# Two decoder layers on one core: linear attention's values and gates become 1024-column units of an ordered instruction list

## The chip, the core and the metric

The kernel runs on one core of one Trainium2 chip. The metric is the time of one execution in microseconds of device time; less is better. Three runs of the kernel before gave 2152.7, 2152.89 and 2154.03 us, median 2152.89.

## What is computed

Two layers over 256 tokens of width 2048, all in float32. One input projection feeds two groups of heads, gated linear attention (chunks of 64 tokens) and stick-breaking attention; their outputs go through one output projection; an MLP with a squared ReLU follows. Cut to what matters here:

```python
def hybrid_layer(x, ...):
    h = rms_norm(x, attn_norm)
    g_q, g_k, g_v, g_gate, g_lr, s_q, s_k, s_v = split(h @ w_in)   # 512 512 1024 1024 16 1024 1024 1024
    log_a = log_sigmoid(g_lr @ w_gate_up + b_gate) / 16
    o_gla = rms_norm(gla_chunked(g_q, g_k, g_v, log_a), gla_out_norm) * silu(g_gate)
    o_sb = rms_norm(stick_breaking_attention(norm(s_q), norm(s_k), s_v), sb_out_norm)
    x = x + concat(o_gla, o_sb) @ w_o
    return x + square(relu(rms_norm(x, mlp_norm) @ w_up)) @ w_down
```

## The kernel before, in words

**Matmuls.** Every float32 operand is split into a high part and a low part of the reduced matmul type: ScalarE copies the high part (`high`, L966 in the list, L570 outside), VectorE subtracts it from the original (`low`, L970 and L571). A product is then three matmuls: high by high, high by low, low by high. Each weight matrix is read once, in blocks of 1 MB.

**Units of the list.** `listed` (L786) handles most of the work as *units* of 1024 output columns and 2048 rows. A unit goes over 8 *pairs*, each of 2 x 128 rows. A plain pair is 2 row blocks x 2 halves of the columns x 2 token halves, so 8 products or 24 matmuls, in two steps of 12. A *quick* pair is multiplied as a 2 x 2 block matrix with 7 products, so 21 matmuls, in four steps; for it VectorE first adds weight blocks (`t13`, `t2`, `t4` in `steps`, L985), the activations need extra sums (`forms`, L429), and after the last quick pair of a unit the partial results are combined (`sums_of`, L1094, and `finals`, L1117). Which pairs are quick stands in `FAST` and `QUICK` (L410, L413), the order of the pairs in `HEADS` and `ORDER`. Step numbers k count through a unit; dictionaries such as `TURNS` say behind which step a piece of other work is put on TensorE.

**The planner.** A list is built as pieces with an engine, a length and dependencies (`Plan`, L40). TensorE's and SP's pieces keep their given order; VectorE's and ScalarE's get due times counted back from TensorE's order and are run in order of due time. The result is written out as a fixed order of instructions on TensorE, VectorE and ScalarE. SP (the DMA queue) and POOL (GpSimd), and the place of a list's instructions among those traced before it, are left to the framework's scheduler.

**One layer in time.** (1) A list for the keys (`sk`) and values (`sv`) of stick-breaking; for layer 0 it is the front list, for layer 1 the tail of layer 0's list. (2) The attention stage, written without a planner: `unit` (L576, 512 columns or less, 96 matmuls for 512) and `unit_t` (L599, transposed output) for the low-rank gate, the queries of stick-breaking, and the linear attention's queries and keys. Each takes 1/8 or 1/4 of its rows and then ticks a counter; `after(n, fn)` hangs a piece of attention work n ticks ahead. `sb_heads(1, ..., (6, 10))` (L1653) is the second half of stick-breaking: scores of its two pairs of heads at ticks 6 and 10, weights 3 ticks later, outputs 1 later, the turned operand 3 later. (3) Still in this manner: the linear attention's values as two units of 512 columns, the turning of the decayed keys (`turn_k`), `gla_pair` (states and scores of a pair of heads, L1693) and `gla_out` (outputs, L1735), and the first half of the gates as a unit of 512 columns. (4) The layer's list: the second half of the gates as kind `"g"` (96 plain matmuls), the gate functions (`gate`, L1256: three logs' steps, a minimum, an exponent, a product for each token half), the output projection as two units `o`, then eight units `up` and `down` of the MLP in turn, then `sk` and `sv` of the next layer.

**Memory.** `acts` is a pool of 19 tiles of 4 KB per partition for activations, the residual `xb` has 4 such tiles of its own (L341) and stays on the chip throughout. Temporary pools of the attention stage and of the lists share one range of addresses; a new tile there waits for the old ones it lies on. The four newest weight blocks have a place (`RAWS`), their split parts five (`RING`).

The lines that set the sets of quick pairs and the stage's values:

```python
413     QUICK = (((5, 6), (5, 6, 7)), ((4, 5, 6), (4, 5, 6)))      # layer 0: sk, sv; layer 1: sk, sv
805     units = [("sk", 0, 0), ("sv", 0, 0)] if front else [("g", 0, 0), ("o", 0, 0), ("o", 0, 1)]
1759    for g in range(2):
            v = values(unit(hT, wl, 0, C_GV + g * 512, 512), tmp("v4", [P, NT, 512], bufs=2))
            for hp in range(2):
                after(1 + 3 * hp, lambda e=2 * g + hp, v=v, c=hp * 2 * P: gla_pair(e, v, c))
        ug = unit(hT, wl, 0, C_GG, 512)
```

Of the kernel before, what the change touches and what calls it, by code (L numbers as in the profile page):

```python
# [10 lines left out]
F32 = mybir.dt.float32  # L11
# [140 lines left out]
def trunk_kernel(  # L152
# [27 lines left out]
    xpool = ctx.enter_context(tc.tile_pool(name="resid", bufs=1, side="right"))  # L180
    apool = ctx.enter_context(tc.tile_pool(name="acts", bufs=19))
# [42 lines left out]
    ATT = ("v4", "tri", "nones", "wg", "reset", "gmask", "mask16", "lr", "lrT", "ha", "hh", "hl", "hA", "on", "dec", "S", "kdz", "row", "bc")  # L224
# [21 lines left out]
    ident16 = cpool.tile([P, P], BF16, name="ident16")  # L246
    kdz = {}
    lc = {}

    def layer_constants():  # L250
        for key in ("tri", "nones"):
            lc[key] = tmp(key, [P, P], F32R, bufs=1)
# [15 lines left out]
        gmask = lc["gmask"] = tmp("gmask", [P, CHUNK], bufs=1)  # L268
        nc.gpsimd.memset(gmask, 1.0)
        for half in range(2):  # L270
# [6 lines left out]
        reset = lc["reset"] = tmp("reset", [P, T], bufs=1)  # L277
        nc.gpsimd.memset(reset, 1.0)
        nc.gpsimd.memset(
            reset.rearrange("p (n c) -> p n c", c=CHUNK)[:, :, 0:1], 0.0  # L280
        )
        kdz["t"] = tmp("kdz", [P, 3, 512], bufs=1)
        nc.gpsimd.memset(kdz["t"], 0.0)

    def build_constants():
        nc.vector.tensor_copy(ident16, ident)

        layer_constants()
# [52 lines left out]
    xb = [xpool.tile([P, NT, 512], F32, name=f"xb{n}") for n in range(4)]  # L341
# [3 lines left out]
    def load_x(n, c=0, w=512):  # L345
        nc.sync.dma_start(xb[n][:, :, c : c + w], xv[:, :, n * 512 + c : n * 512 + c + w])
# [45 lines left out]
    class Operand:  # L392
# [25 lines left out]
    ORDER = {"g": (0, 1, 2, 3), "up": (0, 1, 2, 3, 4, 5, 6, 7), "down": (0, 1, 2, 3, 4, 5, 6, 7)}  # L418

    TURNS = (  # L420
        {1: ((2, 5), (3, 7)), 3: ((1, 1),), 4: ((5, 6), (4, 5)), 7: ((6, 7), (7, 1))},
        {0: ((5, 5),), 1: ((6, 7),), 3: ((4, 1), (7, 6))},
    )
    KEYS = (
        {19: ((0, 0, 5), (0, 1, 7)), 20: ((1, 0, 1),), 21: ((1, 1, 6),)},
        {18: ((0, 0, 5),), 19: ((0, 1, 7),), 20: ((1, 0, 1),), 21: ((1, 1, 6),)},
# [56 lines left out]
    def operand_parts(op, n, h2, key, l, place):  # L483
# [5 lines left out]
        def turn():  # L489
            pt = place()  # L490
            for j in range(2):
                for tt in range(NT):
                    c = (2 * h2 + j) * P
                    nc.tensor.transpose(
                        pt[:, j * T + tt * P : j * T + (tt + 1) * P],
                        xb[n][:, tt, c : c + P], ident,
                    )
# [22 lines left out]
    def norm_squares(n, ssq):  # L520
        for tt in range(NT):
            junk = tmp("t2", [P, 512], bufs=4)
            nc.scalar.activation(
                junk, xb[n][:, tt, :], AF.Square, accum_out=ssq[:, tt, n : n + 1]
# [166 lines left out]
    def sb_scores(qT, kT, h):  # L691
# [11 lines left out]
        for j in range(2):  # L703
            for o in (zA[:, j * T : j * T + P], zB[:, j * P : (j + 1) * P]):
                nc.tensor.matmul(
                    o, ident16, lc["mask16"], start=False, stop=(j == 1), skip_group_check=True
# [79 lines left out]
    def listed(l, front, mixed=None, ons=None, ug=None):  # L786
# [18 lines left out]
        units = [("sk", 0, 0), ("sv", 0, 0)] if front else [("g", 0, 0), ("o", 0, 0), ("o", 0, 1)]  # L805
        fl = l if front else l + 1
        if not front:
            units += [(k, q, n2) for q in range(4) for k in ("up", "down") for n2 in range(2)]
            if fl < DEPTH:
                units += [("sk", 0, 0), ("sv", 0, 0)]  # L810

        def pair_order(u):

            if units[u][0] in HEAD_KINDS:
                i = HEAD_KINDS.index(units[u][0])
                return HEADS[fl][i], set(QUICK[fl][i])
            if units[u][0] != "o":
# [3 lines left out]
            if units[u][2] == 0:  # L821
                return (4, 5, 6, 7, 0, 1, 2, 3), {0, 1}
            return (4, 5, 6, 0, 7, 1, 2, 3), {0, 1}
# [62 lines left out]
        def weights(u, i):  # L886
            kind, q, n2 = units[u]
            if kind in HEAD_KINDS:
                c0 = C_SK if kind == "sk" else C_SV
                src = w_in[fl][2 * i * P : (2 * i + 2) * P, c0 : c0 + 1024]  # L890
            elif kind == "g":
                src = wl[4 * i * P : (4 * i + 4) * P, C_GG + 512 : C_GG + 1024]
# [10 lines left out]
        def load(u, i):  # L903
# [4 lines left out]
            def fn():  # L908
# [4 lines left out]
                dst = box[0]  # L913
                if units[u][0] == "g":
                    dst = dst.rearrange("p k (c n) -> p (k c) n", c=2)
                nc.sync.dma_start(dst, weights(u, i))
# [68 lines left out]
        def steps(u, j, is_fast, r, ld, readers):  # L985
# [3 lines left out]
                "g": hT_now, "o": mixed, "up": hm, "down": up.get(q), "sk": hT, "sv": hT,  # L989
# [5 lines left out]

            if kind == "g":
                for s in range(2):
                    yield parts(
                        lambda s=s: r()[:, s, :].rearrange("p (c n) -> p c n", c=2),
                        readers, ld,  # L1000
                    ), [(m, [(blk(k, tt, 2 * j + s), k) for k in range(2)])
                        for tt, m in enumerate((1, 6))]
                return
# [31 lines left out]
            def fourth():  # L1035
# [16 lines left out]
                (5, [(ext(3) if op is hT or kind == "up" and j == KEPT else blk(0, 1), 0)]), (7, [(ext(2), 1)]),  # L1052
# [31 lines left out]
        def seeds(u):  # L1084

            n2 = units[u][2]
            for m, c, tt in ((2, 0, 0), (4, 0, 1), (3, 1, 0), (8, 1, 1)):
                def seed(m=m, src=xb[2 * n2 + c][:, tt, :]):
                    banks[m] = bank(m)
                    nc.scalar.activation(banks[m], src, AF.Copy)  # L1090
# [40 lines left out]
        def down_tail(u):  # L1131
# [6 lines left out]
            def half(c, p):  # L1138
# [3 lines left out]
                def store(tt):  # L1142
                    if end:
                        nc.sync.dma_start(
                            ov[:, tt, n * 512 : (n + 1) * 512], xb[n][:, tt, :]
# [663 lines left out]
```

## Time and profile before

| | |
|---|---|
| median of 3 runs | 2152.89 us |
| the profiled execution | 2152.91 us |
| its span, first to last instruction | 2151.2 us |
| TensorE, VectorE, ScalarE, GpSimd busy | 100, 88, 65, 2% of the span |
| TensorE's mean granted clock | 0.999 of full speed |
| DMA | 408.98 MB, 55.7% of the 16 engines' time |

The stages lie in the span so: front list 5 to 99 us; layer 0's attention stage to 213, values and first gates to 294, second gates and output projection to 404, MLP to 1082, next keys and values to 1167; layer 1 in the same order, its MLP from 1472 to the end. A row of windows gives, for a stretch, its length and each engine's busy time with the number of instructions, then the granted clock, the share of the DMA engines and GB/s. A row of the chain gives start, length and what the end of the kernel hung on there. A row of lines gives the group and its count, then busy us, mean ns of one, and the idle time ahead of it.

### The profile page before, as it was taken

The numbers are of one execution on the slowest core, as the hardware profiler recorded it, in microseconds if no ns is written. First come the engines' busy times: TensorE is split into PE (matmuls) and PEld (weight loads), VectorE is DVE, ScalarE is ACT, GpSimd is POOL, SyncE is SP. The second block draws the span as 40 slices with busy tenths as digits, with TensorE's granted clock in tenths as the row PEclk, the third lists the DMA queues.
The fourth block names the chain that finished last, engine by engine and source line by source line (L and its number), as shares of the span: only waits on it lengthen the run. The fifth ranks groups of instructions, "written<-read, shape, count | busy, mean of one in ns | idle before, by whom it ended". The sixth has DMA issues, their size and how long they took to land.

```text
span 2151.2 us, 27397 instructions
## 1 busy us (share of the span) xinstructions
PE 2143.1 (100%) x10277; PEld 1787.7 (83%) x10277; DVE 1890.4 (88%) x2355; ACT 1403.8 (65%) x2057; POOL 42.7 (2%) x74
## 2 busy tenths in 40 slices
PE   9999999999999999999999999999999999999999
PEld 7888888888888888888888888888888888888887
DVE  7867569999999899899997775799999999998997
ACT  7676466666576567576666854666665665765674
POOL 0010000000000000000001200000000000000000
PEclk9999999999999999999999999999999999999999
DMA  7554455555556555556655544555555555565564
GB/s 256 159 179 155 157 196 176 193 203 192 199 194 222 188 196 203 208 183 209 208 168 156 181 152 158 192 181 197 212 183 206 205 189 203 191 224 185 196 206 146
DMA packets 136376, 408.98 MB, mean 190 GB/s; under 512 B 6602, under 2 KB 31762, under 8 KB 136244
## 3 DMA queue, kind: packets, MB, share of 16 engines
q1 hardware_dynamic: 136244, 407.24, 55.7%
q8 instruction: 80, 1.31, 0.2%
q14 instruction: 52, 0.43, 0.1%
HBM read 405.12 MB, written 2.10 MB: 189 GB/s over the span
## 4 chain that ended last, share of the span: by engine, by line
PE 94%; ACT 1%; DVE 1%; issue 0%; POOL 0%
PE acc L587 4%; PE acc L593 3%; PE acc L590 3%; PE acc L612 2%; PE acc L616 1%; PE m__623_2954 L1068 1%; PE m__2629_12333 L1068 1%; PE m__2625_12320 L1068 1%; PE m__619_2941 L1068 1%; PE m__2726_12854 L1068 0%; PE m__655_3136 L1068 0%; PE m__2661_12515 L1068 0%; PE m__720_3475 L1068 0%; PE m__2731_12878 L1068 0%; PE m__725_3499 L1068 0%; PE m__2728_12864 L1068 0%
## 5 line engine op out<-in xcount | busy, mean ns | idle before, releaser
L966 ACT ACTIVATE whi<-raw 128x1024 fp32r<-128x1024 f32 (+1 forms) x658 | 684.4, 1056 | 350.9 <-issue 21.1
L970 DVE TENSOR_TENSOR wlo<-raw,whi 128x1024 fp32r<-128x1024 f32 (+1 forms) x658 | 787.6, 1219 | 27.3 <-ACT whi L966 19.0
L571 DVE TENSOR_TENSOR wlo<-raw,whi 128x1024 fp32r<-128x1024 f32 (+2 forms) x128 | 141.7, 1108 | 82.3 <-ACT whi L570 81.1
L966 ACT ACTIVATE whi<-ts 128x1024 fp32r<-128x1024 f32 x129 | 136.6, 1059 | 95.5 <-PE m__1062_5033 L1068 6.5
L970 DVE TENSOR_TENSOR wlo<-ts,whi 128x1024 fp32r<-128x1024 f32 x129 | 158.0, 1225 | 42.5 <-ACT whi L966 42.5
L570 ACT ACTIVATE whi<-raw 128x1024 fp32r<-128x1024 f32 (+2 forms) x128 | 122.0, 954 | 110.7 <-PE acc L593 85.3
L799 DVE TENSOR_TENSOR ts<-raw 128x1024 f32<-128x1024 f32 x129 | 157.6, 1221 | 0.5
L587 PE MATMUL acc<-whi,act 128*128 128x512 f32 (+2 forms) x384 | 140.4, 366 | 0.1
L593 PE MATMUL acc<-whi,act 128*128 128x512 f32 (+2 forms) x384 | 136.5, 356 | 0.0
L590 PE MATMUL acc<-wlo,act 128*128 128x512 f32 (+2 forms) x384 | 136.2, 355 | 0.0
L966 ACT ACTIVATE whi<-t 128x512 fp32r<-128x512 f32 x129 | 80.9, 627 | 49.3 <-DVE t L799 20.2
L970 DVE TENSOR_TENSOR wlo<-t,whi 128x512 fp32r<-128x512 f32 x129 | 88.7, 688 | 9.6 <-ACT whi L966 9.6
L612 PE MATMUL acc<-act,whi 128*128 128x512 f32 x256 | 92.0, 400 | 0.0
L799 DVE TENSOR_TENSOR t<-raw 128x512 f32<-128x512 f32 x129 | 88.9, 689 | 1.1
L799 DVE TENSOR_TENSOR raw<-ts,raw 128x512 f32<-128x512 f32 x129 | 88.6, 687 | 0.3
L587 PEld LDWEIGHTS acc<-whi,act 128*128 128x128 f32 x384 | 72.4, 189 | 13.3 <-issue 2.7
L593 PEld LDWEIGHTS acc<-whi,act 128*128 128x128 f32 x384 | 72.3, 188 | 10.5
L590 PEld LDWEIGHTS acc<-wlo,act 128*128 128x128 f32 x384 | 72.5, 189 | 8.9
L616 PE MATMUL acc<-act,wlo 128*128 128x256 f32 x256 | 71.8, 281 | 0.0
L1199 ACT ACTIVATE act<-act,st 128x512 f32<-128x512 f32 x64 | 44.5, 718 | 32.7 <-DVE act L799 32.7
L612 PEld LDWEIGHTS acc<-act,whi 128*128 128x128 f32 x256 | 48.1, 188 | 10.3
L616 PEld LDWEIGHTS acc<-act,wlo 128*128 128x128 f32 x256 | 48.4, 189 | 0.1
(2583 smaller groups left out, 5480.1 us busy)
## 6 DMA issues: line engine op xcount, KB each, us to landing
raw<-in_w_up_dram SPq DMA_DIRECT2D x128, 1024.0 KB, 5.0
raw<-in_w_down_dram SPq DMA_DIRECT2D x128, 1024.0 KB, 5.3
raw<-in_w_in_dram SPq DMA_DIRECT2D x87, 1024.0 KB, 5.3
raw<-in_w_o_dram SPq DMA_DIRECT2D x32, 1024.0 KB, 5.2
raw<-in_w_in_dram SPq DMA_DIRECT2D x8, 544.0 KB, 3.8
raw<-in_w_in_dram SPq DMA_DIRECT2D x8, 512.0 KB, 3.8
out_dram<-xb SPq DMA_DIRECT2D x8, 256.0 KB, 2.9
xb<-in_x_dram SPq DMA_DIRECT2D x3, 512.0 KB
```

The source lines that it names most:

```text
L570: newest["hi"] = nc.scalar.activation(hi[:, :, :width], r, AF.Copy).ins
L571: newest["lo"] = nc.vector.tensor_tensor(lo[:, :, :width], r, f32(hi[:, :, :width]), ALU.subtract).ins
L587: nc.tensor.matmul(o, xh[:, sl], whi[:, j, :width], start=(k == 0), stop=False)
L590: nc.tensor.matmul(o, xh[:, sl], wlo[:, j, :width], start=False, stop=False)
L593: nc.tensor.matmul(o, xl[:, sl], whi[:, j, :width], start=False, stop=(k == KT - 1))
L612: nc.tensor.matmul(acc[f], whi[:, j, sl], op.both(k), start=(k == 0), stop=False, skip_group_check=True,)
L616: nc.tensor.matmul(acc[f][:, T:], wlo[:, j, sl], xh, start=False, stop=(k == KT - 1), skip_group_check=True,)
L799: nc.vector.tensor_tensor(dst, a, b, op)
L966: nc.scalar.activation(box["h"][:, :n], src(), AF.Copy)
L970: nc.vector.tensor_tensor(box["l"][:, :n], src(), f32(box["h"][:, :n]), ALU.subtract)
L1068: nc.tensor.matmul(o, lhs, rhs, start=start and k == 0, stop=end and i + 1 == len(blocks) and k == 2, skip_group_check=onto,)
L1199: nc.scalar.activation(box[h][:, tt, :], box[h][:, tt, :], AF.Relu, scale=rr[:, tt : tt + 1],)
```

## The change

- The linear attention's values (`gv`) become a third unit of 1024 columns behind `sk` and `sv` in the list ahead of the attention stage, with quick pairs 5, 6, 7 in layer 0 and 5, 6 in layer 1. They stay in two activation tiles until the layer's list.
- Both halves of the gates become one unit `gg` of 1024 columns at the head of the layer's list, with quick pairs 5 and 6.
- The turning of the decayed keys, states, scores, outputs, their norms and the gating become pieces of that list at places that `LINEAR` names.
- The second half of stick-breaking begins at ticks 5 and 8 in place of 6 and 10.
- The residual has no pool of its own; it takes 4 tiles of `acts`, which grows from 19 to 23. It is stored to a buffer in device memory at the end of layer 0, and loaded again ahead of the output projection in both layers (in layer 0 from the input).
- The orders of pairs and turns in the keys', values' and output projection's units are new. The sets of quick pairs there are the same.
- A few constants change pool; `kz`, the cleared tile of turned keys, is filled on POOL at the head of the list.

```diff
-    xpool = ctx.enter_context(tc.tile_pool(name="resid", bufs=1, side="right"))
-    apool = ctx.enter_context(tc.tile_pool(name="acts", bufs=19))
+    apool = ctx.enter_context(tc.tile_pool(name="acts", bufs=23))
...
-    HEAD_KINDS = ("sk", "sv")
-    QUICK = (((5, 6), (5, 6, 7)), ((4, 5, 6), (4, 5, 6)))
+    HEAD_KINDS = ("sk", "sv", "gv")
+    QUICK = (
+        ((5, 6), (5, 6, 7), (5, 6, 7), (5, 6)),
+        ((4, 5, 6), (4, 5, 6), (5, 6), (5, 6)),
+    )
     HEADS = (
-        ((0, 2, 1, 3, 5, 6, 4, 7), (4, 0, 5, 1, 6, 7, 3, 2)),
-        ((0, 2, 5, 3, 6, 4, 1, 7), (6, 0, 7, 5, 4, 1, 2, 3)),
+        ((0, 3, 1, 4, 5, 6, 2, 7), (0, 1, 5, 2, 7, 6, 4, 3), (5, 4, 2, 3, 6, 7, 0, 1), (1, 2, 3, 6, 5, 0, 4, 7)),
+        ((0, 1, 5, 6, 3, 4, 7, 2), (6, 1, 2, 4, 5, 3, 7, 0), (0, 5, 3, 6, 7, 4, 1, 2), (1, 2, 3, 6, 5, 0, 4, 7)),
     )
+    LINEAR = {
+        ('gg', 0, 1): (('k', 0, 6),),
+        ('gg', 0, 2): (('k', 1, 6),),
+        ('gg', 0, 4): (('pair', 3, 1, 6), ('pair', 2, 7, 5)),
+        ('gg', 0, 14): (('out', 2, 1),),
+        ('gg', 0, 15): (('pair', 0, 1, 5),),
+        ('gg', 0, 16): (('out', 3, 7),),
+        ('gg', 0, 17): (('out', 0, 1),),
+        ('o', 0, 0): (('pair', 1, 1, 7),),
+        ('o', 0, 2): (('out', 1, 1),),
+        ('o', 0, 3): (('turn', 0, 7),),
+        ('o', 0, 4): (('turn', 3, 6),),
+        ('o', 0, 6): (('turn', 2, 1), ('turn', 1, 7)),
+    }
+    OUT = ((5, 6, 4, 3, 0, 2, 1, 7), (6, 7, 0, 2, 4, 1, 3, 5))
...
-        units = [("sk", 0, 0), ("sv", 0, 0)] if front else [("g", 0, 0), ("o", 0, 0), ("o", 0, 1)]
+        heads = [(kind, 0, 0) for kind in HEAD_KINDS]
+        units = heads if front else [("gg", 0, 0), ("o", 0, 0), ("o", 0, 1)]
...
+            def half(c, p):
+                for tt, a in enumerate(finals(box, c, p, lambda tt: box[c][:, tt, :])):
+                    def scale(tt=tt):
+                        gates_t[c] = box[c]
+                        nc.scalar.activation(
+                            box[c][:, tt, :], box[c][:, tt, :], AF.Copy,
+                            scale=st["now"][:, tt : tt + 1],
+                        )
+
+                    gate_done[c, tt] = add("ACT", A1, scale, a)
+                gate(c)
...
+            a = add("PE", 6 * 0.112, states, k_done, free[m])
+            b = add("DVE", 0.9, carry, a)
+            free[m] = [b]
+            c = add("PE", 4 * 0.12, scores, free[m2])
+            d = add("DVE", 0.8, masked, c)
+            free[m2] = [d]
...
+            a = add("PE", 1.2, out, b, d, free[m])
+            a = add("ACT", A1 + 2.0, take, a)
+            free[m] = [a]
+            a = add("DVE", 0.2, mean, a)
+            a = add("ACT", 0.4, root, a)
+            a = add("DVE", 0.5, step, a)
+            on_done[e] = add("DVE", V1, lambda: mul_heads(ons[e], ons[e], root_mean, 4), a)
...
+            kd_done = add("DVE", 2.4, None, add("ACT", 1.3, None, add("PE", 0.0, None)))
+            kz = tmp("sx2", [P, 3, 512], bufs=NX["sx", 2])
+            nc.gpsimd.memset(kz, 0.0)
...
+            if kind == "o" and n2 == 0:
+                for n in range(4):
+                    x_done[n] = [add(
+                        "SP", 1.5, lambda n=n: load_x(n, src=xs if l else None), lag=4.6
+                    )]
...
+                if kind == "down" and q == 3 and not end:
+                    held_back.append(lambda: add("SP", 1.5, lambda: store_x(n), x_done[n]))
...
+                if j == order[3]:
+                    while held_back:
+                        held_back.pop(0)()
...
-        sb_heads(1, qT, kTs[1], vs[1], (6, 10))
+        sb_heads(1, qT, kTs[1], vs[1], (5, 8))
```

## Rows read from the trace of the kernel before

**Rows 1.** The page: busy time of the engines, and the chain by engine.
```profile
PE 2143.1 (100%) x10277; PEld 1787.7 (83%) x10277; DVE 1890.4 (88%) x2355; ACT 1403.8 (65%) x2057; POOL 42.7 (2%) x74
...
PE 94%; ACT 1%; DVE 1%; issue 0%; POOL 0%
```
**Rows 2.** Waits of TensorE: who for whom, us in total, times, longest.
```profile
PE m__36_171 L1068 <- ACT whi L966: 1.4, 1, 1.4
...
PE m__36_171 L1068 <- DVE wlo L970: 0.5, 1, 0.5
PE ps L766 <- ACT hA L735: 0.5, 2, 0.2
```
**Rows 3.** Windows by stage of layer 0: PE, PEld, DVE, ACT, POOL, clock, DMA.
```profile
4.92:99.19 94.27, 92.30 (x418) 75.35 (x418) 84.03 (x123) 69.36 (x135) 5.10 (x13) 0.98 0.62 213
99.19:212.65 113.46, 112.94 (x709) 100.04 (x708) 77.96 (x124) 80.25 (x181) 14.46 (x17) 1.00 0.55 172
212.65:294.08 81.43, 81.43 (x463) 66.41 (x461) 43.22 (x71) 37.87 (x76) 1.23 (x4) 1.00 0.47 155
294.08:403.79 109.71, 109.71 (x501) 91.15 (x500) 98.31 (x129) 75.50 (x107) 0.00 (x0) 1.00 0.58 197
403.79:1082.00 678.21, 678.21 (x3073) 563.08 (x3072) 647.07 (x746) 448.66 (x558) 0.00 (x0) 1.00 0.58 199
```
**Rows 4.** Chain in the output projection: first and last of 12 like pieces.
```profile
316.93 1.36 PE m__655_3136 L1068 x6
...
331.89 1.36 PE m__663_3176 L1068 x6
```
**Rows 5.** Chain around a pair of the linear attention in the values' unit.
```profile
267.93 0.81 PE ps L1700 x12
268.74 0.44 PE ps L1717 x8
269.18 0.43 PE acc L587
...
274.86 0.89 PE ps L1742 x8
275.75 1.02 PE ps L1750 x12
```
**Rows 6.** Lines of ScalarE from 212.65 to 340 us, shapes apart.
```profile
L966 ACT ACTIVATE whi<-raw 128x1024 fp32r<-128x1024 f32 x19 | 19.4, 1051 | 7.4 <-PE m__663_3176 L1068 3.1 <-PE m__623_2954 L1068 2.9 <-PE m__658_3152 L1068 1.4
L637 ACT ACTIVATE t<-act 128x128 f32<-128x128 f32 x16 | 4.8, 299 | 0.1
L637 ACT ACTIVATION_READ_ACCUMULATOR t<-act 128x1 f32 x16 | 3.0, 188 | 0.0
...
L1266 ACT ACTIVATE t<-t 128x512 f32<-128x512 f32 x4 | 2.5, 635 | 0.1
...
L756 ACT ACTIVATE act<-ps 128x512 f32<-128x512 f32 x4 | 2.4, 601 | 10.4 <-PE ps L1750 10.4
...
L627 ACT ACTIVATE t<-acc 128x256 f32<-128x256 f32 x2 | 0.8, 380 | 1.5 <-PE acc L616 1.5
```
**Rows 7.** Lines of VectorE from 212.65 to 340 us, shapes apart.
```profile
L970 DVE TENSOR_TENSOR wlo<-raw,whi 128x1024 fp32r<-128x1024 f32 x18 | 21.4, 1221 | 0.6 <-ACT whi L966 0.4
...
L799 DVE TENSOR_TENSOR act<-act,t 128x512 f32<-128x512 f32 x4 | 2.7, 686 | 0.0
...
L629 DVE TENSOR_TENSOR t<-acc,t 128x256 f32<-128x256 f32 x2 | 0.8, 422 | 0.4 <-ACT t L627 0.4
```
**Rows 8.** Timeline of ScalarE ahead of the list (294 us): start, length, idle before.
```profile
288.60 0.60 ACT L756 ACTIVATE act<-ps 128x512 f32<-128x512 f32 x1 [7.78 <-PE ps L1750]
...
291.10 3.90 ACT L966 ACTIVATE whi<-raw 128x1024 fp32r<-128x1024 f32 x4
```
**Rows 9.** Window in the start; columns as in rows 3.
```profile
9.20:12.40 3.20, 3.20 (x9) 2.49 (x8) 1.30 (x2) 2.40 (x7) 0.00 (x0) 0.50 1.03 418
```
**Rows 10.** Waits of SP's queue: its longest in total.
```profile
SPq L916 <- DVE wlo L970: 1413.2, 301, 11.2
```

More of the change, by code (lines that the diff above doesn't have):

```diff
@@ L784, in trunk_kernel, with listed @@
     st = {}
-    def listed(l, front, mixed=None, ons=None, ug=None):
+    def listed(l, front, mixed=None, old=None, linear=None):
         wl = w_in[l]
@@ L1354, in g_tail, with gates_tail, sums @@
-        def g_tail(p):
-            gate_copies(1, lambda tt: banks[(1, 6)[tt]], lambda tt: p[(1, 6)[tt]])
-            for tt, m in enumerate((1, 6)):
-                free[m] = [gate_done[1, tt]]
+        def gates_tail(u):
+            box = {}
+            def sums(p):
+                sums_of(box, p)
+            def half(c, p):
[5 more added lines that the diff above has]
+                            scale=st["now"][:, tt : tt + 1],
+                        )
+                    gate_done[c, tt] = add("ACT", A1, scale, a)
+                gate(c)
+            return sums, half
@@ new lines, in turned_k, with turn, copy @@
+        def turned_k(tt, m):
+            kd = linear[1]
+            def turn():
+                pk = banks[m] = bank(m)
+                for e in range(4):
+                    nc.tensor.transpose(
+                        pk[:, e * P : (e + 1) * P], kd[:, e, tt * P : (tt + 1) * P], ident
+                    )
+            def copy():
+                for half in range(2 - tt):
+                    ps = slice(half * CHUNK, (half + 1) * CHUNK)
+                    nc.vector.tensor_copy(kz[ps, 2 * tt + half, :], banks[m][ps, :])
+            a = add("PE", 4 * TR, turn, kd_done, free[m])
+            k_done.append(add("DVE", 1.2 - 0.6 * tt, copy, a))
+            free[m] = k_done[-1:]
@@ L1470, in listed @@
                         begin = m not in begun
[L1471 to L1474 removed]
+                        end = final if m in (2, 4, 3, 8) else [j] == lasts
                         begun.add(m)
@@ L1549, in trunk_kernel @@
         for c in range(2):
-            vs[c] = values([vs[c]()[:, tt, :] for tt in range(NT)], tmp("v4", [P, NT, 512], bufs=2))
+            vs[c] = values([vs["sv", c]()[:, tt, :] for tt in range(NT)], tmp("v4", [P, NT, 512], bufs=2))
         def sb_heads(g, qT, kT, v, first):
@@ L1759, in trunk_kernel @@
-        for g in range(2):
-            v = values(unit(hT, wl, 0, C_GV + g * 512, 512), tmp("v4", [P, NT, 512], bufs=2))
-            for hp in range(2):
-                after(1 + 3 * hp, lambda e=2 * g + hp, v=v, c=hp * 2 * P: gla_pair(e, v, c))
-        ug = unit(hT, wl, 0, C_GG, 512)
         assert not held
         open_scope("sbuf", mlp=1)
-        kTs, vs = listed(l, False, mixed, ons, ug)
+        kTs, vs = listed(l, False, mixed, vs, (ke, kd, qz))
 _INS = [
```

395 lines of the change are left out of this document (194 added, 201 removed).

## The prediction

> **What bounds the kernel now.** I read the page first. TensorE has instructions in flight for the whole span, and the chain that ended last lies on it for 94% [rows 1]. "Busy" is not enough, since pipelined matmuls cover each other, so I next asked what TensorE waited for: 1.4 and 0.5 us for the first weights, 0.5 us in the two attention stages, and nothing else once the first weights are there [rows 2]. Then the stages [rows 3]: only the front list (94.27 us, TensorE busy 92.30) and the attention stage (113.46 against 112.94) show idle TensorE. In the stretch that the change rewrites (values, gates, output projection) and in the MLP the two figures are equal. VectorE is the next engine: 95% busy in the MLP (647.07 of 678.21 us), yet only 53% in the values stretch (43.22 of 81.43). So the time is the sum of TensorE's work, and an edit is worth what it takes from or adds to that sum, as long as its operands come in time. Last I took the price of that work from the chain of waits: in the list six matmuls of 512 columns advance the end by 1.36 us, in the first piece and in the twelfth alike [rows 4], 0.2267 us each.
>
> The profiled execution took 2152.91 us (span 2151.2, the rest lies around it), the median of three runs is 2152.89; I take the sum from 2152.9.
>
> **Matmuls removed.** Before, values and gates of one layer are four pieces of 512 columns, 96 matmuls each: 384. After, they are two units of 1024 columns with 8 pairs of 24 matmuls, where a quick pair has 7 products of 3, so 21. Layer 0 has three quick pairs in the values and two in the gates (183 + 186 = 369), layer 1 two and two (186 + 186 = 372). The keys' and values' quick sets of stick-breaking stay as large as they were, and so does the output projection's. Gone are 15 + 12 = 27 matmuls, at 0.2267 us **6.1 us**.
>
> The TensorE page of the Trainium skill ("TensorE: Matmul & The Clock Gate", section "Back-to-back issue gap") gives other prices, 216 ns for an isolated gap of 512 columns and about 131 ns sustained; by these the term would be 5.8 or 3.5 us. The trace disagrees with the second: 1.36 us for six, at full clock, is 227 ns, and I stay with it.
>
> **Small matmuls, moved.** States, scores, outputs and transposes of the four head pairs are the same instructions; only their place changes. What a place costs is in the chain [rows 5]: 12 state matmuls 0.81, 8 score matmuls 0.44, then the next big matmul 0.43 instead of 0.23; outputs 0.89 + 1.02, and 0.43 again for the big one behind. Before, eight such entries per layer cost 0.20 us each. After, pairs 3 and 2 stand back to back, so one entry of 0.20 goes; the turning of kd, cut into pieces in the values unit, stands whole in the list. I take the one entry, 0.20 x 2 layers = **0.4 us**; at worst 0, at best twice that.
>
> **VectorE and ScalarE behind it.** Over values, gates and output projection VectorE now does 43.22 + 98.31 = 141.5 us [rows 3]. Out go 32 low-part splits at 1.22 (39.0) [rows 7]. In come, for the gates' unit, 12 splits (14.6), two quick pairs at 3 x 1.22 + 0.69 for their four low parts and 1.22 + 2 x 0.69 for the sums of weights (2 x 6.95 = 13.9), and the unit's combining, 2 x 0.69 + 1.22 + 4 x 0.69 = 5.4: together 33.9. That leaves 136.4 us over a TensorE time of 191.1 - 43.5 (values' 192 matmuls) - 1.4 (the gates' 6) - 0.4 = 145.8 us, 94%. The MLP carries 95% without a wait. ScalarE falls below VectorE: 113.4 - 33.6 (32 splits at 1.05 [rows 6]) - 2.5 (four copies at 0.63) + 20.8 (12 + 6 splits, two of 0.63, one copy) = 98.1 us, 67%. The front list takes the values' unit (about 34 to 39 us of VectorE in 42) with no deadline behind it.
>
> The crowd is local: from the gates' last quick pair to the turn of operand 1 (13 steps, 36 us of matmuls, with pieces and turns 48 us) ScalarE has 13 splits at 1.05, four reads of an output with its squares at 0.60 + 4 x (0.30 + 0.19) = 2.56, and four gate chains of 5 x 0.63 = 3.2, 36.7 us; with roots and operand copies about 41 of 48. The last gate chain after the gates' last matmul is two combines, scale, three logs, minimum, exponent and product, twice for the two token halves, some 10 us; TensorE arrives at the turn that needs it 5 steps and three pieces later, 17.7 us. So it fits, with little to spare. I bound the new waits from below by 0 (the MLP's rows) and from above by one late split (1.05 + 1.22 = 2.3 us) at three places per layer, 13.8 us; nearest is the MLP at 95%, so I take **0.8 us**. Below nothing is excluded, since a wait cannot be negative and the old ones in this stretch were nil.
>
> **Edits at nothing.** Residual in the general pool: 19 tiles + 4 become 23, the same bytes. New transfers: x is read again in both layers and stored once, 2 MB each. They go into SP's queue ahead of the output projection's first weights and, the stores, behind the fourth load of the next keys' unit. At the 418 GB/s of the start [rows 9] that is 5 us of queue per 2 MB. The cover is that the queue waits for buffers, not the other way round: 1413.2 us of SP's waits end with a low-part split [rows 10], and the DMA engines' share in the stretch is 0.58 [rows 3]. If the cover were gone, 5 us per layer. x is needed only at the combining of the output projection's quick pairs, over 40 us later. A load that finds no free tile would hold the weights behind it; by my count of live tiles (11 operand, 4 mixed, 2 + 2 + 2) two are free when the gates begin and every pair used frees more. Masks, kz and per-layer constants on POOL: POOL is 2% busy [rows 1]. The new order of pairs and turns at the start: same loads in the same order; between -1 and +1 us, taken as 0.
>
> **Sum:** 2152.9 - 6.1 - 0.4 + 0.8 = **2147.2 us** (-0.26%). About 0.2%, 4.3 us, is what a measurement of this kernel can tell from no change; faster means below 2148.6, slower above 2157.2.
>
> **Rivals.** *A, slower: the seam behind the key projection.* In the kernel before, ScalarE idled 7.78 us at the end of the gates' first half and then took the last output's read before the list's first split [rows 8]. After, what stands last in front of the list is the joining of the keys, which waits for TensorE's last key matmul. If the list's splits queue behind it, TensorE waits in each layer for two copies (0.38 each [rows 6]), two adds (0.42), two products (0.69) and the low split (1.22) [rows 7]: 4.2 us end to end. Against it: the first split had a reason of its own to be late, its buffers lay over values that the last output still read; now nothing read late lies there. At the start the granted clock stood at 0.50, the 1.2 GHz level, from 9.2 to 12.4 us [rows 9], after TensorE's waits of 1.4 and 0.5 us, which cost half of 3.2 us. The same here makes 5.8 us per layer, 2152.9 - 6.5 + 11.6 = 2158.0. It decides from 5.4 us per layer on. The same page of the Trainium skill (Part 1) says that an idle TensorE falls back to 1.2 GHz; the trace agrees at the start, and shows waits of 0.2 us without it.
> *B: the gates' chain is late.* If the last chain stands behind the first gates' 6.4 us and two reads in ScalarE's queue, turn 3 comes 2 to 4 us late per layer: 2146.4 + 2 x 3 = 2152.4. For it speaks the crowd above, against it the list's order, which is computed by due times.
> *C: stick-breaking's last two pairs*, whose scores start one and two steps earlier, make the second pair's scores and the first pair's weights meet in one step, where they share banks. One late exponent there costs what the two waits of [rows 2] and a read of the bank do, 1 to 2 us per layer: 2149.4.
> That the matmuls don't go is no rival: their number is fixed by the sets of quick pairs.
>
> **How the numbers follow.** Forecast 0.70, A 0.10, B 0.13, C 0.07. Faster: the forecast's 0.70 and a little of C, 0.71. Slower: A and B's far end, 0.11. Same: 0.18. The range reaches from 2144.8 (no new waits, 1 us gained at the start, the small matmuls' best) to 2152.6 (all of C, half of B); outside are A, half of B and a few chances below. The forecast's own range is 2144.8 to 2148.6.
>
> **What would show it.** The list's matmuls still 1.36 us per six; TensorE's waits no longer than now, none behind the key projection; VectorE near 94% from gates to output projection; in the old units' lines 96 matmuls of 512 columns per layer, where 384 stand now. Wrong would be: a clock below 1.00 after 14 us, ScalarE idle before the first gate split, a wait of TensorE for a gated operand, or a front list that grows by more than the 41.5 us of its new unit.

## The result and the profile after

The changed kernel takes 2161.32 us (median of 7 runs, 2158.94 to 2163.17), the kernel before in the same comparison 2153.62 (7 runs, 2152.63 to 2154.12): ratio 1.0035, 95% interval 1.0024 to 1.0047. The forecast was 2147.2, faster, in a range of 2144.8 to 2152.6. The change is slower by 7.7 us, its fastest run lies above the slowest of the kernel before, and the prediction was wrong.

The profiled execution of the changed kernel has a span of 2159.6 us, 8.4 more than before. The page, as in [rows 1]:

```profile
PE 2142.6 (99%) x10250; PEld 1786.5 (83%) x10250; DVE 1943.1 (90%) x2429; ACT 1421.0 (66%) x2079; POOL 41.5 (2%) x71
```

The 27 matmuls are gone (10277 to 10250), VectorE does 53 us more and ScalarE 17. But TensorE is busy for less of a longer span. Its longest waits, where the kernel before has four lines in all (three of them in [rows 2]):

```profile
PE m__38_167 L1079 <- ACT whi L985: 3.3, 2, 1.9
PE m__595_2648 L1079 <- DVE wlo L989: 1.6, 1, 1.6
PE m__2634_12098 L1079 <- DVE wlo L989: 1.6, 1, 1.6
PE ps L562 <- POOL ident masks.py:199: 1.5, 1, 1.5
PE m__595_2648 L1079 <- ACT whi L985: 1.4, 1, 1.4
PE m__2634_12098 L1079 <- ACT whi L985: 1.4, 1, 1.4
PE m__38_167 L1079 <- DVE wlo L989: 0.9, 2, 0.7
PE ps L789 <- ACT hA L758: 0.5, 2, 0.2
PE m__763_3564 L1079 <- ACT m__763_3564 L1101: 0.3, 1, 0.3
```

Two places are new: a second wait in the front list (`m__38`, two times now), and one in each layer (`m__595`, `m__2634`: the first product of the gates' unit, right behind the key projection). The windows by stage of layer 0, columns as in [rows 3]: front list with the values' unit, attention stage, gates and output projection, MLP.

```profile
4.96:147.08 142.12, 137.72 (x601) 112.55 (x601) 120.53 (x159) 92.55 (x160) 1.37 (x3) 0.98 0.61 205
147.08:260.84 113.76, 113.37 (x709) 100.18 (x708) 75.07 (x124) 79.15 (x181) 18.34 (x28) 1.00 0.55 172
260.84:410.60 149.76, 146.46 (x762) 120.38 (x761) 137.14 (x202) 100.39 (x170) 0.00 (x0) 1.00 0.54 184
410.60:1088.80 678.20, 678.20 (x3074) 563.16 (x3073) 647.22 (x746) 449.19 (x558) 0.00 (x0) 1.00 0.58 201
```

The MLP and the attention stage are what they were (678.20 and 113.76 us against 678.21 and 113.46). The front list took 142.12, where 94.27 and the new unit's 41.5 make 135.8: 6.3 too much. Gates and output projection took 149.76, where 145.8 was worked out: 4.0 too much. In layer 1 the same stretch took 151.37, 5.6 too much:

```profile
1329.51:1480.88 151.37, 148.07 (x762) 121.50 (x761) 137.13 (x202) 100.52 (x170) 0.00 (x0) 0.99 0.54 182
```

Inside the list nothing has changed its price. The chain of waits around an output of the linear attention, as in [rows 4] and [rows 5]:

```profile
295.37 1.36 PE m__599_2661 L1079 x6
296.73 0.89 PE m__658_2930 L1471 x8
297.62 1.02 PE m__658_2930 L1479 x12
298.64 1.59 PE m__600_2668 L1079 x6
```

Six matmuls are 1.36 us, the output 0.89 and 1.02, and the entry behind it 0.2.

**The loss at the start.** The timelines of ScalarE and TensorE there (start, length, idle before):

```profile
18.00 0.84 ACT L526 ACTIVATE act<-m__54_231,gcol_a 128x256 fp32r<-128x256 f32 x2 [0.48 <-PE m__54_231 L517]
18.73 1.06 ACT L985 ACTIVATE whi<-raw 128x1024 fp32r<-128x1024 f32 x1
```

```profile
17.36 0.60 PE L517 MATMUL m__54_231<-ident,act 128*128 128x128 f32 x4
19.83 0.53 PE L1079 MATMUL m__38_167<-whi,act 128*128 128x512 f32 x1 [1.88 <-ACT whi L985]
21.09 0.80 PE L1079 MATMUL m__38_167<-wlo,act 128*128 128x512 f32 x1 [0.73 <-DVE wlo L989]
```

The split at 18.73 is the first of the second pair's weights. It stands behind the copy of that pair's own turned operand (`m__54`), and TensorE did that turn at 17.36, directly ahead of the matmuls that need both. So nothing covers a copy, a split and a low split (VectorE's low part of the weights): TensorE starts this pair's matmuls at 19.83 and has the low part at 21.09. In the kernel before the second pair was turned two steps earlier. The time from one matmul's start to the next, above the full-clock step of its shape, summed over the first 50 us (entries of 0.15 us and more), is 11.2 us; before it was 5.0.

Behind this wait the clock falls to half clock (0.50, the 1.2 GHz level), as it did at the start before [rows 9]. It falls again behind layer 1's seam:

```profile
21.69:25.95 4.26, 4.26 (x11) 3.20 (x10) 2.84 (x3) 2.16 (x4) 0.00 (x0) 0.50 0.76 234
1334.28:1337.60 3.32, 3.32 (x9) 2.59 (x8) 3.32 (x4) 0.79 (x2) 0.00 (x0) 0.50 1.00 323
```

**The loss at the seam.** The window behind layer 0's last key matmul, then ScalarE's and VectorE's timelines there:

```profile
260.84:264.35 3.51, 0.77 (x3) 0.19 (x1) 3.02 (x5) 3.51 (x6) 0.00 (x0) 1.00 0.11 19
```

```profile
258.33 0.69 ACT L794 ACTIVATE act<-ps,gcol_b 128x512 fp32r<-128x512 f32 x1 [6.04 <-PE ps L789]
260.81 0.73 ACT L650 ACTIVATE t<-acc 128x256 f32<-128x256 f32 x2 [1.78 <-PE acc L639]
261.43 4.84 ACT L985 ACTIVATE whi<-raw 128x1024 fp32r<-128x1024 f32 x5
```

```profile
261.22 0.77 DVE L652 TENSOR_TENSOR t<-acc,t 128x256 f32<-128x256 f32 x2 [1.41 <-ACT t L650]
262.10 0.69 DVE L1833 TENSOR_TENSOR act<-t,act 128x512 f32<-128x512 f32 x1
262.71 0.68 DVE L1834 TENSOR_TENSOR act<-t,act 128x512 f32<-128x512 f32 x1
263.31 5.76 DVE L989 TENSOR_TENSOR wlo<-raw,whi 128x1024 fp32r<-128x1024 f32 x5
```

ScalarE idles 1.78 us for TensorE's last key matmul, copies, and only then starts the list's splits; VectorE adds and multiplies before the first low split. Between the starts of TensorE's matmuls 1.6 and 1.8 us are lost, 3.4 in each layer. This is rival A, instruction for instruction.

### The profile page after: what moved, and what is told of

The parts are those of the page before. It is cut to its first block, busy times and chain, and to the rows that moved or that the text cites. A ratio compares the mean times of both kernels' runs of the same rounds, so it can differ in the third digit from the quotient of the medians.

```text
span 2159.6 us, 27484 instructions
## 1 busy us (share of the span) xinstructions
PE 2142.6 (99%) x10250; PEld 1786.5 (83%) x10250; DVE 1943.1 (90%) x2429; ACT 1421.0 (66%) x2079; POOL 41.5 (2%) x71
## 4 chain that ended last, share of the span: by engine, by line
PE 97%; DVE 1%; ACT 1%; DMA 0%; issue 0%; SPq 0%; POOL 0%; DVEq 0%; ACTq 0%
PE acc L635 2%; PE acc L610 1%; PE acc L613 1%; PE acc L616 1%; PE acc L639 1%; PE m__2638_12111 L1079 0%; PE m__2639_12118 L1079 0%; PE m__2634_12098 L1079 0%; PE m__600_2668 L1079 0%; PE m__595_2648 L1079 0%; PE m__2728_12607 L1079 0%; PE m__689_3157 L1079 0%; PE m__763_3564 L1079 0%; DMA act<-in_x_dram 0%; PE m__2802_13014 L1079 0%; PE m__599_2661 L1079 0%
## 5 line engine op out<-in xcount | busy, mean ns | idle before, releaser
L985 ACT ACTIVATE whi<-raw 128x1024 fp32r<-128x1024 f32 (+1 forms) x706 | 735.8, 1058 | 391.6 <-issue 28.5
L989 DVE TENSOR_TENSOR wlo<-raw,whi 128x1024 fp32r<-128x1024 f32 (+1 forms) x706 | 843.2, 1215 | 28.9 <-ACT whi L985 20.2
L989 DVE TENSOR_TENSOR wlo<-ts,whi 128x1024 fp32r<-128x1024 f32 x138 | 168.6, 1222 | 41.8 <-ACT whi L985 41.0
L594 DVE TENSOR_TENSOR wlo<-raw,whi 128x1024 fp32r<-128x1024 f32 (+2 forms) x80 | 82.8, 1036 | 40.7 <-ACT whi L593 40.0
L593 ACT ACTIVATE whi<-raw 128x1024 fp32r<-128x1024 f32 (+2 forms) x80 | 71.2, 892 | 47.8 <-PE acc L616 22.9
L610 PE MATMUL acc<-whi,act 128*128 128x272 f32 (+2 forms) x192 | 62.8, 327 | 0.0
L613 PE MATMUL acc<-wlo,act 128*128 128x272 f32 (+2 forms) x192 | 61.5, 320 | 0.0
L616 PE MATMUL acc<-whi,act 128*128 128x272 f32 (+2 forms) x192 | 61.4, 320 | 0.0
L493 DVE TENSOR_TENSOR act<-act,act 128x512 fp32r<-128x512 f32 x64 | 42.4, 684 | 0.0
L489 ACT ACTIVATE act<-act 128x512 fp32r<-128x512 f32 x64 | 39.1, 624 | 0.5
L610 PEld LDWEIGHTS acc<-whi,act 128*128 128x128 f32 x192 | 36.4, 190 | 3.6 <-issue 0.7
```

Of the source, the lines that this page charges most:

```text
L493: nc.vector.tensor_tensor(lo, src, f32(h), ALU.subtract)
L593: newest["hi"] = nc.scalar.activation(hi[:, :, :width], r, AF.Copy).ins
L594: newest["lo"] = nc.vector.tensor_tensor(lo[:, :, :width], r, f32(hi[:, :, :width]), ALU.subtract).ins
L610: nc.tensor.matmul(o, xh[:, sl], whi[:, j, :width], start=(k == 0), stop=False)
L613: nc.tensor.matmul(o, xh[:, sl], wlo[:, j, :width], start=False, stop=False)
L616: nc.tensor.matmul(o, xl[:, sl], whi[:, j, :width], start=False, stop=(k == KT - 1))
```

## The experiments

Times are medians; "stalls" are the sums named above, by the profiled execution. The kernel before had a median from 2152.8 to 2153.0 us in these comparisons.

### e_start: the old order of pairs and turns alone

```diff
-        ((0, 3, 1, 4, 5, 6, 2, 7), ...
+        ((0, 2, 1, 3, 5, 6, 4, 7), ...
-        {1: ((1, 5),), 2: ((2, 7),), 3: ((3, 1),), 4: ((5, 6), (4, 5)), 6: ((6, 7),), 7: ((7, 1),)},
+        {1: ((2, 5), (3, 7)), 3: ((1, 1),), 4: ((5, 6), (4, 5)), 7: ((6, 7), (7, 1))},
```

> The changed kernel with one part undone: in layer 0's keys the pairs and their turns stand again in the order of the kernel before (second pair 2, turned behind step 1), all else as changed; the first two 1 MB weight loads still stand ahead of the second block of x in SP's queue. Theory T (order of turns: the second pair's turn stands right ahead of its matmuls, and the splits of its weights queue on ScalarE behind the copy of that turn): the 2.0 and 1.0 us waits at 17.7 to 21 us and the second half-clock stretch behind them go, the front list ends about 6 us sooner, time about 2155. Theory Q (order of the queue: x's second block comes late because two 1 MB loads went ahead of it): the turn behind step 1 now waits some 3 us for x, the loss moves and does not go, time 2158 to 2161.

Measured: 2163.33 us (2157.89 to 2164.01, 4 runs), no better than the change itself and above what either theory gave; the profiled execution is the fastest of the four, and it has no half clock behind the seams. The waits for weights are gone and one for x has come:

```profile
PE m__46_193 L517 <- DMA act<-in_x_dram: 3.1, 1, 3.1
```

So theory Q's mechanism holds here: the loss moved. The stalls of the first 50 us are 9.1 us. SP's queue in the change and, below it, in the kernel before (start and length of the issue):

```profile
4.18 1.38 SPq L935 DMA_DIRECT2D raw<-in_w_in_dram  x2
5.60 1.08 SPq L345 DMA_DIRECT2D act<-in_x_dram  x2
```

```profile
4.17 0.43 SPq L346 DMA_DIRECT2D xb<-in_x_dram  x1
4.65 0.47 SPq L916 DMA_DIRECT2D raw<-in_w_in_dram  x1
```

Before, x's second block was issued first and the second pair's weights behind it; after, two 1 MB blocks go first. The chain of waits of the changed kernel shows what that costs, from issue to landing:

```profile
5.60 9.83 DMA act<-in_x_dram
```

The Trainium skill ("DMA: Bandwidth & Descriptors", section "Queues, rings and completion order") says that each of the DMA engines takes a ring's descriptors in order; the 9.83 us behind two megabytes agree with that.

### e_spq: the old order of the queue alone

```diff
-        with tc.manual_schedule(engines=MANUAL):
+        with tc.manual_schedule(engines=MANUAL | {mybir.EngineType.SP} if front else MANUAL):
```

> The changed kernel with the other half undone: SP's queue in the front list in the list's own order, so that x's second block stands ahead of the second pair's weights as in the kernel before; pairs and turns as changed. Theory T: the turn of the second pair still stands behind step 3, TensorE still waits about 3 us in front of its matmuls and falls to half clock again, time 2160 to 2161. Theory Q: the loss goes, the front list ends about 6 us sooner, time about 2155.

Measured: 2159.32 us (2156.89 to 2162.39, 9 runs); TensorE waits for no load of x, and its waits for ScalarE's splits are those of the change (`m__38`, 3.3 us in two waits).

Theory T holds here, stalls 9.9 us. Each order by itself is enough to lose most of the time, which is why undoing one shows so little.

### e_startspq: both

It holds both edits above.

> Both of the two edits above in one kernel: pairs and turns of layer 0's keys and SP's queue in the front list as in the kernel before. Both theories: the stalls of the first 50 us are those of the kernel before (about 5.0 us where the changed kernel has 11.2), time about 2155. If the start still lost 3 us or more, neither order would be the cause, and the tiles that x now shares with the operands would be.

Measured: 2157.30 us (2154.41 to 2158.57, 10 runs), 2.3 above the expected 2155; stalls in the first 50 us 4.7, as expected. The start is whole again, and what is left is the seam, with half clock behind it in both layers of this profile: 6.4 us at layer 0's seam and 4.8 at layer 1's.

### e_xown: why the queue changed

```diff
-    apool = ctx.enter_context(tc.tile_pool(name="acts", bufs=23))
+    xpool = ctx.enter_context(tc.tile_pool(name="resid", bufs=1, side="right"))
+    apool = ctx.enter_context(tc.tile_pool(name="acts", bufs=22))
...
-            xt[n] = act_tile(F32, (P, NT, 512))
+            own = n == 1 and src is None and not xt.get(("own", n))
+            xt["own", n] = True
+            xt[n] = xpool.tile([P, NT, 512], F32, name=f"xb{n}") if own else act_tile(F32, (P, NT, 512))
```

> The changed kernel with the keys' pairs and turns of the kernel before (as in the first run), and the second block of x in layer 0 in a tile of its own in place of one of the general pool (22 + 1 tiles); SP's queue left to the framework. With that tile the load of x's second block stands ahead of the second pair's weights again. If the move of the residual into the general pool is what put it behind them, TensorE's wait of 3.3 us for x at 12 us goes and the stalls of the first 50 us are near 5 us: about 4 us less than the run with the turns alone, time 2155 to 2157 (the seams stay as changed). If not, the wait for x stays near 3 us.

Measured: 2157.26 us (2154.59 to 2158.81, 10 runs), 6 less than e_start. In the profiles 3.4 of these are the start (stalls 5.7 us for 9.1); where the others lie was not traced, since e_start's profile is that of its fastest run. SP's queue has x's second block first again:

```profile
4.17 0.44 SPq L348 DMA_DIRECT2D xb<-in_x_dram  x1
4.65 1.52 SPq L938 DMA_DIRECT2D raw<-in_w_in_dram  x2
```

So the move of this block of x into the general pool is what put its load back: from e_start to here nothing but its tile and the pool's size differ. What in the framework's scheduler makes it so was not tried.

### e_seam3: the joining of the keys as a piece of the list

```diff
-            t = join(unit_t(hT, wl, C_GK + b * 256))
+            acc = unit_t(hT, wl, C_GK + b * 256)
+            if b == 1:
+                break
+            t = join(acc)
...
-            kd_done = add("DVE", 2.4, None, add("ACT", 1.3, None, add("PE", 0.0, None)))
+            kd_high = add("ACT", 1.3, join_copies, add("PE", 0.0, None))
+            kd_done = add("DVE", 2.4, join_sums, kd_high)
+            whi[3].append(kd_high)
+            wlo[3].append(kd_done)
...
-        sb_heads(1, qT, kTs[1], vs[1], (5, 8))
+        sb_heads(1, qT, kTs[1], vs[1], (5, 7))
```

> The changed kernel with the joining of the last keys (two copies, two adds, two products) made a piece of the layer's list, placed behind the list's third split, and the second half of stick-breaking one tick earlier in its second pair (5, 7), so that nothing late stands ahead of the splits on ScalarE. The start stays as changed. Theory A (the list's splits queue behind the joining, which waits for TensorE's last key matmul): the two waits of 1.6 and 1.8 us behind the key projection fall to under 0.7 us together in each layer, no half-clock stretch follows in layer 1, time 2161.3 - 2 x 3 - 1.6 = 2153.7, from 2152.5 to 2155. Rival (the first split waits for GpSimd's fills, which end about 259.8 us, or for its weights): the waits stay at 3 us or more, time 2160 to 2162.

Measured: 2154.55 us (2152.61 to 2156.25, 10 runs), 6.8 below the change. TensorE loses 1.2 and 1.4 us at the two seams in place of 3.4, and no half clock follows in the profile, which is of the fastest of these runs. Theory A holds, though the waits do not fall below 0.7. What is left is the first weights themselves:

```profile
257.04 3.91 ACT L985 ACTIVATE whi<-raw 128x1024 fp32r<-128x1024 f32 x4 [3.76 <-DMA raw<-in_w_in_dram]
```

### e_all: the three edits together

It holds the edits of e_start, e_spq and e_seam3.

> The changed kernel with both orders at the start as in the kernel before, and the joining of the last keys as a piece of the list behind its third split (with stick-breaking's second pair one tick earlier). If the two losses add up, start 11.2 to 4.7 us of stalls (-6.5) and the seams 3.4 to 1.3 us per layer with no half-clock stretch (-6.8 measured in the seam's run): 2161.3 - 6.5 - 6.8 = 2148.0, from 2147 to 2149.5, faster than the kernel before. If something else costs time (VectorE's crowd, the transfers of x), it stays above 2150.

Measured: 2149.17 us (2148.50 to 2150.03, 11 runs), ratio to the kernel before 0.9982 (0.9974 to 0.9991). The losses add up, and the change is now faster than the kernel before by 3.8 us. Of the seams 1.0 and 1.4 us are left.

### e_all_r: and the first tiles from the general rings

```diff
-                if x % RAWS < RAWS - 3:
+                if x % RAWS == (0 if front else RAWS - 1):
...
-                if i % RING < RING - 4:
-                    return tmp(f"{tag}{4 + i % RING}", [P, 2, 512], F32R, bufs=1)
-                return part_tile(tag, i % RING - (RING - 4) + part_base, [P, 2, 512])
+                if i % RING == (0 if front else RING - 1):
+                    return tmp(f"{tag}4", [P, 2, 512], F32R, bufs=1)
+                return part_tile(tag, i % RING - (1 if front else 0) + part_base, [P, 2, 512])
```

> As the kernel with all three edits, and in a layer's list the first weight block and the first split parts take tiles of the general rings, the ones that lie over the attention stage's tiles come fourth and fifth. Theory: what is left at the seam (0.2 to 0.4 and 1.0 us) comes from the first weight block, which landed only at 257.0 us, 0.8 us before TensorE was free, since its tile waited for the stage ahead; then the first splits are done before TensorE ends the keys and the rest of the wait goes, 2148 - 2 x 1.2 = 2145.6. Rival: ScalarE and VectorE themselves are late (the join and the stick-breaking operand ahead of the splits), the wait moves to a later split and the time stays at 2148.

Measured: **2145.84 us** (2145.65 to 2147.00, 5 runs), ratio 0.9967 (0.9955 to 0.9980): the fastest of all, faster than both kernels. Three splits of the list now end before TensorE's last key matmul; the timeline of ScalarE has the last two of them, and the joining behind them:

```profile
251.35 2.01 ACT L985 ACTIVATE whi<-raw 128x1024 fp32r<-128x1024 f32 x2 [1.58 <-PE acc L635]
253.90 0.73 ACT L1598 ACTIVATE t<-acc 128x256 f32<-128x256 f32 x2 [0.53 <-PE acc L639]
```

TensorE's waits are those of [rows 2] again, with the seeding of the second output unit added (ScalarE copies x into the banks to which that unit's products are then added):

```profile
PE m__38_167 L1079 <- ACT whi L985: 1.4, 1, 1.4
PE ps L789 <- ACT hA L758: 0.5, 2, 0.2
PE m__763_3564 L1079 <- ACT m__763_3564 L1101: 0.3, 1, 0.3
PE m__2802_13014 L1079 <- ACT m__2802_13014 L1101: 0.3, 1, 0.3
PE m__38_167 L1079 <- DVE wlo L989: 0.2, 1, 0.2
```

The window of its gates and output projection: 146.40 us (145.8 worked out), VectorE 133.38, 91%.

```profile
253.80:400.20 146.40, 146.05 (x763) 120.54 (x762) 133.38 (x199) 96.71 (x166) 0.00 (x0) 1.00 0.55 189
```

### e_r58: without the earlier tick

It is e_all_r with `(5, 8)` again.

> The kernel with four edits, with stick-breaking's second pair at the changed kernel's tick 8 again, so that of the seam's edits only the joining as a piece of the list and the first tiles from the rings are left. Theory: the splits stood behind the joining alone, the tick is not needed, no wait over 0.3 us behind the key projection, 2145.8 within 0.6. Rival: the copy of the last stick-breaking operand, one tick before the end, holds ScalarE as well; then waits of about 1 us per layer come back, 2147.5 to 2148.5.

Measured: 2147.08 us (2146.66 to 2147.82, 7 runs), between the two expected times. The profile has no wait at layer 0's seam, 0.6 us for one low split in layer 1, and 1.0 us more of half clock at the start than e_all_r's. The tick is worth little; the joining and the tiles are the cure. The tiles without the joining were not tried.

### e_all_sp_r: the transfers of x

It is e_all_r with SP's queue in the list's order in every list.

> As the kernel with four edits, with SP's queue in the list's own order in every list, so that the four loads of x (2 MB) come behind the gates' eighth weight block, not among the fifth to eighth. If the transfers of x cost time where they stand (queue and bandwidth ahead of the gates' weights), this is 1 to 2 us faster per layer; if they are covered, as the prediction had it, within 0.7 us of the kernel with four edits.

Measured: 2145.91 us (2145.72 to 2146.29, 5 runs), the same as e_all_r. Where the loads of x stand among the gates' weights costs nothing, as predicted; moving them away altogether was not tried.

### e_onequick and e_gv1: the price of the matmuls

One quick pair in place of two or three, in values and gates on e_all (e_onequick), then in the values alone on e_all_r (e_gv1). The edit of e_gv1; in e_onequick the fourth place, the gates', is `(5,)` in both layers too:

```diff
-        ((5, 6), (5, 6, 7), (5, 6, 7), (5, 6)),
-        ((4, 5, 6), (4, 5, 6), (5, 6), (5, 6)),
+        ((5, 6), (5, 6, 7), (5,), (5, 6)),
+        ((4, 5, 6), (4, 5, 6), (5,), (5, 6)),
```

> As the kernel with all three edits, but with one quick pair in place of two or three in the linear attention's values and in the gates: 6 + 3 matmuls more in layer 0 and 3 + 3 in layer 1, 15 in all, and less work for VectorE. By the price of 0.2267 us, 3.4 us slower than the kernel with all three edits (2151.4 if that is 2148.0). If VectorE's crowd behind the quick pairs cost TensorE time, less than 3.4 us, by 1 us or more.

Measured: 2163.75 us (2161.97 to 2165.91, 4 runs), 14.6 above e_all: not a test of the price. With one quick pair the gates' unit has fewer steps, the pieces of `LINEAR` are keyed by step numbers and land elsewhere, and TensorE waits at new places in both layers' lists, for 1.2 us at the longest. It has e_gv1's wait at L610 (below) as well, and half clock at three places.

> The kernel with four edits, with one quick pair in place of three (layer 0) and two (layer 1) in the linear attention's values: 6 + 3 = 9 matmuls more, at places that nothing else is keyed to. By the price of 0.2267 us per matmul 2.0 us slower, 2145.8 + 2.0 = 2147.9, from 2147.3 to 2148.5. If the quick pairs gave less than their price, because VectorE's added work costs TensorE waits, under 1.2 us.

Measured: 2151.36 us (2151.15 to 2152.54, 11 runs), 5.5 above e_all_r and outside the expected range. Nine matmuls more; the starts of all 512-column matmuls add up to 2.25 us more, near the 2.04 of the price. The other 3.4 us lie in one place that no one planned: with another end of the front list the framework put small work of the attention stage (a row and the gains turned, L570 and L306) ahead of its first unit on TensorE,

```profile
PE acc L610 <- ACT whi L593: 1.2, 1, 1.2
...
PE ps L570 <- POOL bc L569: 0.4, 1, 0.4
```

and half clock followed:

```profile
144.39:147.80 3.41, 3.26 (x15) 2.95 (x15) 0.70 (x3) 0.25 (x1) 0.00 (x0) 0.50 0.51 141
```

### e_out: a quick pair earlier

```diff
-    OUT = ((5, 6, 4, 3, 0, 2, 1, 7), (6, 7, 0, 2, 4, 1, 3, 5))
+    OUT = ((5, 6, 4, 3, 0, 1, 2, 7), (6, 7, 0, 2, 4, 1, 3, 5))
```

> The kernel with four edits, with the last quick pair of the first output projection unit one place earlier (pairs 2 and 1 change places). TensorE's wait of 0.5 us per layer for the seeding of the second unit's bank comes from the first unit's combining, which ends late with only one plain pair behind the last quick one. With two plain pairs behind it the wait goes: 1.0 us faster, about 2144.8. Rival: the seeding waits for x or for ScalarE's own queue, and the wait of 0.5 stays, 2145.8.

Measured: 2149.11 us (2148.61 to 2150.25, 11 runs), 3.3 slower than e_all_r, neither of the expected times. The wait for the seeding is gone, so its cause was right. But the quick pair now meets VectorE earlier, and a low split is late in each layer:

```profile
PE m__2721_12563 L1079 <- DVE wlo L989: 1.2, 1, 1.2
PE m__682_3113 L1079 <- DVE wlo L989: 1.2, 1, 1.2
```

This low split runs at 341 us, some 9 us behind the turn of operand 1 with which the prediction's crowd ended. So VectorE can be late in this stretch, but not at the place that the prediction named.

## Why the prediction was wrong

**The work was sized rightly.** e_all_r does the work of the change without its two accidents, and with the first tiles in another place. Its span is 2143.9 us, 7.26 below the kernel before (2151.2): 6.44 in the starts of 512-column matmuls and 0.82 in the rest. The forecast had 6.1 and 0.4 less, 0.8 more. Its median of 2145.84 lies in the forecast's own range of 2144.8 to 2148.6; e_all, which still has part of the seams' waits, lies 0.6 above that range. The 0.8 us for new waits was worked out from no row, only chosen between bounds; that e_all_r has 1.0 us of them is luck, since they stand at a place that no step named (below). VectorE has 137.1 us from the gates to the output projection in the change, 136.4 were worked out.

**The first step that failed** is "the new order of pairs and turns at the start: same loads in the same order; between -1 and +1 us, taken as 0". The loads were not in the same order, and the turns not early enough: 11.2 - 4.7 = 6.5 us of the profile. The first half could be read in the diff: the second pair's operand is turned behind step 3, right ahead of step 4 that needs it, where it had been behind step 1. The second could only be suspected: x's tiles change pool, and SP's order is left to the framework. The prediction looked at the move of x for its bytes and its cover alone. The two faults also hide each other: undoing one gives 9.1 or 9.9 us of stalls against 11.2.

**The second** is the dismissal of rival A. Its mechanism came, in the place named. The argument against it, that nothing read late lies under the first split's buffers, answers another question: the order of ScalarE's and VectorE's instructions in a list is fixed, the joining stood ahead of it, and in the timeline the first split starts at 261.43, when the copies end. Whether a tile is free does not matter to a split that stands behind the joining. [rows 8] had shown the old ending, in which a copy of an output stood in front of the splits with 7.78 us of idle time ahead of it. The price of A was near: 3.4 us for 4.2, and a half clock that adds from nothing to 3.0 us. e_startspq is rival A alone, 2157.3 us where it was given 2158.0. With the start mended it still makes the change slower than the kernel before, ratio 1.0018 (1.0009 to 1.0027); the chance of 0.10 was too small.

**The sum.** From e_all_r to the changed kernel the span grows by 15.7 us: 6.5 at the start, 3.4 at each seam, 1.6 of half clock behind layer 1's, and the remaining 0.8 in small entries. Against the 7.3 gained, that is the 8.4 lost.

**The rest.** Rival B did not come: no wait of TensorE for a gated operand. Nor C: the waits of stick-breaking are 0.5 us as before [rows 2]. The transfers of x are covered (e_all_sp_r). A wait that no step had is the seeding of the second output unit, 0.5 us per layer in starts of matmuls: the combining of the first unit ends late with one plain pair behind its last quick one. Of the list of what would show the prediction wrong, two came in full: a clock below 1.00 after 14 us, and a front list that grew by more than the new unit. A third came in substance: ScalarE idled 1.78 us in front of the copies that stood ahead of the first gate split.

## What to carry to other kernels

When work between two stages is taken away, look at what now stands last in each engine's queue ahead of the next stage: an evacuation that waits for TensorE holds all the splits behind it, and here the cure was to give it to the planner of the next list, behind that list's first splits. An edit may be costed at nothing only after the order of each queue around it has been compared: here a change of pool moved a load behind two megabytes. And where two causes each suffice for a loss, undoing them singly shows little (2.1 and 1.3 us of stalls here, 6.5 together); undo them together before judging either.

## What the runs showed of the hardware

A wait of 3.4 us in two parts, with a single matmul between them, does not always bring half clock. In the profiles of the change, e_start, e_spq, e_startspq and e_xown it happened at ten seams; six had half clock behind them, which cost 1.4 to 3.0 us (0.20 us for each 512-column matmul), four had none, in the same instructions. Behind the waits of 1.0 to 1.4 us in e_seam3 and e_all it came at none of four, but in e_gv1 it came behind waits of 0.4 and 1.2 us. The Trainium skill ("TensorE: Matmul & The Clock Gate", Part 1) has TensorE fall to 1.2 GHz when idle, and calls the cold stretch at a kernel's start variable from run to run. The seams vary likewise, and so does the start: of the kernels that share e_startspq's start, e_all_sp_r has 4 steps of 0.43 us there, e_startspq and e_all_r 5, e_all and e_r58 10.

The kernels with both seams as changed scatter over 4 to 6 us from run to run, e_all_r over 1.4. Half clock that comes or stays away fits that: of the change's seven runs the two longest have a mean granted clock of 0.996, the others 0.998. But only one run of each kernel has a profile.

A granted clock of 1.00 in a window can also mean that the trace holds no record of the clock there. In the changed kernel's first matmuls it reads 1.00, while they start 0.43 us apart, as in [rows 9], where it read 0.50: this trace's first record begins at 13.34 us, that of the kernel before at 5.68, and time without a record counts as full clock. The window, and two lines of TensorE's timeline in it:

```profile
9.05:13.32 4.27, 4.27 (x11) 3.19 (x10) 1.29 (x2) 1.15 (x4) 0.00 (x0) 1.00 1.02 413
```

```profile
9.48 0.63 PE L1079 MATMUL m__40_173<-whi,act 128*128 128x512 f32 x1
9.91 0.63 PE L1079 MATMUL m__40_173<-wlo,act 128*128 128x512 f32 x1
```

The steps between starts are the safer reading.
